# Two layers' block inversions, and some of layer 1's elementwise work, assigned to other engines

## The chip, the core and the metric

The kernel runs on one core of a Trainium2 chip. The metric is the device time of one execution in microseconds (us). The core has five engines that each run their own instructions in order and wait for one another by semaphores: TensorE (PE, with its weight loads shown as PEld), VectorE (DVE), ScalarE (ACT), GpSimd (POOL) and SyncE (SP, which here issues DMAs).

## The reference

The reference is one inference step of a two-layer hybrid decoder with a width of 1024. Layer 0 is a gated DeltaNet: an input projection, a short causal convolution on q, k and v, and a chunked delta rule in which every chunk solves a triangular system. Layer 1 is an RWKV-7 time mixing: five mixtures of a token with the one before it, projections r, k, v and z, a low-rank decay and rate, and a state update that the kernel also handles by chunks with triangular systems.

```
L = jnp.where(strict, jnp.einsum('nbhik,nbhjk->nbhij', kb, k) * decay, 0.0)
A = L + jnp.eye(chunk, dtype=L.dtype)
...
sol = lax.linalg.triangular_solve(A, rhs, left_side=True, lower=True, unit_diagonal=True)
...
xs = xn[None] + xx[None] * mu[:, None, None, :]
rkvz = jnp.einsum('sbtd,sde->sbte', xs[:4], w_rkvz)
...
kk = l2norm((k * k_k).reshape(B, T, H, N))
k = k * (1.0 + (a - 1.0) * k_a)
S = (S * d_t[:, :, None, :]
     + jnp.einsum('bhvk,bhk->bhv', S, -kk_t)[..., None] * b_t[:, :, None, :]
     + v_t[..., None] * k_t[:, :, None, :])
```

16 meta tokens, the prompt of 1024 tokens and 8 sample sequences of 8 tokens make 1104 columns, which the kernel handles in three segments of 384, 384 and 336.

## The kernel before, in words

**Products and splits.** A product in fp32 accuracy is three matmuls of halves: hi by x, lo by x, hi by x's lo. `split` (L135) makes the halves: ACT copies the hi half (L139), and POOL or DVE subtracts it from the value to get the lo half (L143). Weights come in as `wraw` (128 x 512 for half of a 128-column tile), and leave as `whi` and `wlo`.

**The inversions.** Each triangular system is handled as 32x32 blocks along the diagonal, which are inverted, and merged by PE. `inverse_steps` (L681) inverts up to 120 blocks at once, a block to a partition, in 31 steps. Step j makes a product `invtmp` of (31-j) x (j+1) elements to a partition (L689), and subtracts it from rows j+1 to 31 of `invT` (L691). Each of the 62 instructions needs the one before. `inverse_open` sets `invT` to the unit matrix (memsets L677 and L678 on POOL). Layer 0 has eight batches, one for each head pair, with 72 partitions; layer 1 has five, with 120 (the last 96): 13 x 31 = 403 steps.

**The order of layer 0.** The order of instructions on each engine is that in which the program emits them. Layer 0's work is emitted around one long stream of matmuls, the projections. After every six matmuls comes a gap, and a table (`Gaps`) tells which functions are called in it. Head pair j has 72 gaps from 24 + 72 j. In `prep_plan` (L731) the inversion's steps of pairs 1 to 6 are put one in 1.1 gaps, those of pairs 0 and 7 one in 0.8. Behind the last step, one gap apart, come four ACT copies of the inverse (L814), DMAs, and the merges of the system. Meanwhile `conv_plan` runs the convolution of the next tiles: a PE tile is copied to `raw` by ACT (L621), with the three columns before it copied by POOL (L620); ACT scales the first tap (`cvy`, L115), DVE adds the other three (L634), ACT takes a tanh, and DVE makes q, k or v (L641). The recurrence of the head pair before runs too: its `w` (ACT), `X` and `S` and `o` (DVE, L1038, L1071, L1092) lie between PE's `rA` products.

**The order of layer 1's projections.** `projections` (L2370) runs the r, v and z tiles, eight of each, as matmuls of 24 to a segment (`dense_tile`, L1436) with a gap after every 12, and a table `plan` of 180 gaps. `projection_weights` (L2334) gives `fetch` (the DMA) and `cast` (the split) of half a tile's weights; 48 halves are cast, three of them ahead of the first mixing. `mix_steps` (L2315) makes the token-shift mixture `mixs` (scaled on ACT, L2330 on DVE) and splits it, with the lo half alternately on POOL and DVE. `system_steps` (L1566) prepares one of 24 systems of a key head pair and segment; L1583, L1585 and L1592 on POOL are among its steps. Five systems make a batch, whose blocks are inverted by `system_inverse` (L1630), two steps to a gap over 16 gaps, and copied by ACT (L1638); 8 gaps later begin the merges. `late_weights` streams the z and output weights behind (`Stream`, split on POOL).

Of the kernel before, what the change touches and what calls it, by code (L numbers as in the profile page):

```python
# [88 lines left out]
class Builder:  # L89
# [496 lines left out]
    def conv_plan(self, ends, ft, dst, done=None):  # L586
# [75 lines left out]
        for s, e in enumerate(ends):  # L662
# [5 lines left out]
            if done is not None:  # L668
                L.put(e + 8, lambda s=s: done(s), 2.2)
        L.put(ends[2] + 3, ending, 2.5)  # L670
        L.put(ends[2] + 6, store, 3)
        return out
# [7 lines left out]

    def inverse_steps(self, A, nb, pool, T=None):  # L681

        nc = self.nc
        T = self.inverse_open(nb, pool) if T is None else T
        Tv = T.rearrange("p (i j) -> p i j", j=32)
        for j in range(31):
            n, m = 31 - j, j + 1
            tmp = self.t(pool, [128, 256], "invtmp", 1)[0:nb, 0:n * m].rearrange("p (n m) -> p n m", m=m)
            nc.vector.tensor_tensor(tmp, A[:, j, j + 1:32].unsqueeze(2).broadcast_to([nb, n, m]),  # L689
                                    Tv[:, j, 0:m].unsqueeze(1).broadcast_to([nb, n, m]), op=ALU.mult)  # L690
            nc.vector.tensor_tensor(Tv[:, j + 1:32, 0:m], Tv[:, j + 1:32, 0:m], tmp, op=ALU.subtract)  # L691
            yield Tv
# [38 lines left out]
    def prep_plan(self, j, B, G, o, pace):  # L731
# [67 lines left out]
        def invert():  # L799
# [5 lines left out]
            yield  # L805
            inv = self.inverse_steps(c.Av, 72, fp, T)
            for u in range(31):
# [758 lines left out]
    def system_steps(self, Q, B):  # L1566
# [15 lines left out]
        self.act(iD, cs, AF.Exp, scale=self.DEC)  # L1582
        nc.gpsimd.tensor_tensor(kk, kk, iD, op=ALU.mult)  # L1583
        yield
        nc.gpsimd.tensor_scalar(a, a, pc("rwkv_k_a"), self.omka[:, Q.p:Q.p + 1], op0=ALU.mult, op1=ALU.add)  # L1585
        yield
        ssp = self.ps("f", 2, "rss")
        for c in range(6):
            for h in (0, 1):
                b = slice(64 * h, 64 * h + 64)  # L1590
                self.mm(ssp[b, c:c + 1], sq[b, 64 * c:64 * c + 64], self.ones[b, 0:1])
        nc.gpsimd.tensor_tensor(a, a, k, op=ALU.mult)  # L1592
        nc.sync.dma_start(self.ald[Q.n], al)
# [36 lines left out]
    def system_inverse(self, B):  # L1630
# [3 lines left out]
        Av = B.A.rearrange("p (i s) -> p i s", s=32)  # L1634
        inv = self.inverse_steps(Av.rearrange("p i s -> p s i"), nb, pool)
        for Tv in inv:
# [697 lines left out]
    def projection_weights(self):  # L2334
# [11 lines left out]
        def cast(h):  # L2346
            whi[h], wlo[h] = (t(self.wp, [128, 4, 128], x, self.WB, F32R) for x in ("whi", "wlo"))
            self.split(raw.pop(h), whi[h], wlo[h])
        for h in (0, 1):
            fetch(h)  # L2350
        for h in (0, 1):
            cast(h)
            fetch(h + 2)
        cast(2)
        fetch(4)
        return tiles, whi, wlo, fetch, cast
# [13 lines left out]
    def projections(self, xa, xb, ip, opened, tiles, whi, wlo, fetch, cast):  # L2370
# [8 lines left out]
        def put(g, f, late=2):  # L2379
            plan[g].append((late, f))  # L2380
# [7 lines left out]
        def mixed(g, m, k, s, u):  # L2388
            c0, n = SEGS[s]
            if m == 3 and s == 2:  # L2390
                dst = [f[:, x, k, 0:n] for x in (0, 1)]
            else:
                dst = [x[k][:, c0:c0 + n] for x in xs[m]]
            g_ = self.mix_steps(m, k, SEGS[s], xb[k], dst, "pool" if u % 2 else "dve")
            steps(g, g_, 2)

        starts, g = [], 0
        for m, k in tiles:
            starts.append(g)
            g += 2 * count(m, k)  # L2400
        for h in range(3, 48):
            g = starts[h // 2]
# [3 lines left out]
            else:  # L2406
                put(max(0, g - 1) if h > 3 else 5, lambda h=h: cast(h), 0)
                put(g + 1 if h > 3 else 7, lambda h=h: h + 2 < 48 and fetch(h + 2), 0)

# [72 lines left out]

        for ti, (m, k) in enumerate(tiles):
            dst = {0: self.rd, 2: self.vd, 3: self.zd}[m]
            for s, (c0, n) in enumerate(SEGS[0:count(m, k)]):
                w = Halves(whi, 2 * ti), Halves(wlo, 2 * ti)
# [140 lines left out]
```

## Time and profile before

| | us |
|---|---|
| median of 3 runs | 2273.2 (2270.88 to 2274.19) |
| the profiled execution's own time | 2271.0 |
| its span | 2269.3 |
| PE busy | 2143.4 |
| DVE busy | 1584.5 |
| ACT busy | 1250.7 |
| POOL busy | 1004.0 |

The granted clock of PE is 0.98 on average. A page shows for every group of instructions the line, the engine, the operation, the tiles out<-in with their shapes, how many there are, busy time in us and the mean of one in ns, and behind a second bar the idle time of the engine just ahead of them with what ended it. A view of waits shows which engine, at which line, waited for which other: us in total, times, longest. A view of windows shows busy times in stretches of the span. A row of the timeline has the start, the length, the engine and the instruction, and in brackets the idle time before it.

### The profile page before, as it was taken

The numbers are of one execution on the slowest core, as the hardware profiler recorded it, in microseconds if no ns is written. First come the engines' busy times: TensorE is split into PE (matmuls) and PEld (weight loads), VectorE is DVE, ScalarE is ACT, GpSimd is POOL, SyncE is SP. The second block draws the span as 40 slices with busy tenths as digits, with TensorE's granted clock in tenths as the row PEclk, the third lists the DMA queues.
The fourth block names the chain that finished last, engine by engine and source line by source line (L and its number), as shares of the span: only waits on it lengthen the run. The fifth ranks groups of instructions, "written<-read, shape, count | busy, mean of one in ns | idle before, by whom it ended". The sixth has DMA issues, their size and how long they took to land.

```text
span 2269.3 us, 55274 instructions
## 1 busy us (share of the span) xinstructions
PE 2143.4 (94%) x20382; PEld 1966.5 (87%) x20382; DVE 1584.5 (70%) x4167; ACT 1250.7 (55%) x3631; POOL 1004.0 (44%) x1385
## 2 busy tenths in 40 slices
PE   7889999999999999989999999898999999999997
PEld 6788889889898989878999999798889977788886
DVE  6778788796969687885435762559887637667765
ACT  5536565556556565645433464644545456676763
POOL 4416262534335252614341442464543345566663
PEclk9999999999999999999999999999999999999997
DMA  3324242424333342436344234577786676655532
GB/s 113 79 67 127 65 124 67 110 80 109 85 105 99 81 122 71 114 78 184 95 143 106 70 103 169 167 237 196 206 247 155 157 186 155 173 162 158 168 118 91
DMA packets 495400, 291.61 MB, mean 129 GB/s; under 512 B 222345, under 2 KB 480506, under 8 KB 495130
## 3 DMA queue, kind: packets, MB, share of 16 engines
q1 hardware_dynamic: 495130, 288.08, 45.2%
q8 instruction: 161, 2.64, 0.5%
q14 instruction: 109, 0.89, 0.1%
HBM read 195.66 MB, written 92.30 MB: 127 GB/s over the span
## 4 chain that ended last, share of the span: by engine, by line
PE 46%; DVE 28%; issue 7%; ACT 6%; DMA 6%; POOL 3%; SPq 3%; DVEq 0%; POOLq 0%; ACTq 0%
PE d L129 10%; DVE invtmp L689 5%; PE rA L133 5%; DVE invT L691 5%; DVE cvy L634 4%; PE dz L129 4%; PE zo L129 3%; PE do L129 3%; PE rA L129 3%; PE dv L129 2%; PE fG L129 2%; PE dk L129 1%; DMA wraw<-in_gdn_w_out 1%; POOL wlo L143 1%; DVE E L765 1%
## 5 line engine op out<-in xcount | busy, mean ns | idle before, releaser
L143 POOL TENSOR_TENSOR wlo<-wraw,whi 128x512 fp32r<-128x512 f32 x238 | 321.1, 1350 | 490.1 <-ACT whi L139 391.5
L634 DVE SCALAR_TENSOR_TENSOR cvy<-raw,cw,cvy 128x408 f32<-128x408 f32 (+2 forms) x288 | 180.0, 625 | 35.8 <-ACT cvy L115 30.5
L689 DVE TENSOR_TENSOR invtmp<-invA,invT 72x31 f32<-72x31 f32 (+31 forms) x403 | 189.0, 469 | 15.6 <-POOL invT L678 10.1
L129 PE MATMUL d<-xc,whi 128*128 128x384 f32 (+1 forms) x640 | 181.4, 344 | 6.7 <-ACT xc L139 2.9
L691 DVE TENSOR_TENSOR invT<-invT,invtmp 72x31 f32<-72x31 f32 (+31 forms) x403 | 176.6, 438 | 14.1 <-DVE invtmp L689 0.2
L115 ACT ACTIVATE raw<-cvy 128x408 f32<-128x408 f32 (+2 forms) x96 | 49.8, 518 | 226.2 <-DVE cvy L634 178.0
L139 ACT CAST whi<-wraw 128x512 fp32r<-128x512 f32 x238 | 145.3, 612 | 26.0 <-DMA wraw<-in_rwkv_w_rkvz 12.5
L129 PE MATMUL dv<-xc,whi 128*128 128x384 f32 (+1 forms) x480 | 154.6, 343 | 0.0
L129 PE MATMUL dz<-xc,whi 128*128 128x384 f32 (+1 forms) x480 | 153.2, 342 | 0.0
L129 PEld LDWEIGHTS d<-xc,whi 128*128 128x128 f32 x640 | 118.0, 191 | 10.5 <-ACT xc L139 3.5
L129 PE MATMUL d<-xc,wlo 128*128 128x384 f32 (+1 forms) x320 | 105.4, 339 | 1.9 <-POOL wlo L143 1.8
L129 PE MATMUL d<-xa,whi 128*128 128x384 f32 (+1 forms) x336 | 101.2, 344 | 3.4 <-ACT whi L139 1.6
L129 PE MATMUL dz<-xa,whi 128*128 128x384 f32 (+1 forms) x288 | 102.3, 355 | 0.7 <-DVE zg L905 0.7
L129 PE MATMUL dv<-xa,whi 128*128 128x384 f32 (+1 forms) x288 | 100.9, 350 | 0.0
L1929 POOL TENSOR_SCALAR y<-y,mv,grs 128x64 f32<-128x64 f32 x132 | 81.1, 632 | 34.7 <-DVE grs L164 29.4
L129 PEld LDWEIGHTS dz<-xc,whi 128*128 128x128 f32 x480 | 90.4, 191 | 0.9
L129 PEld LDWEIGHTS dv<-xc,whi 128*128 128x128 f32 x480 | 89.0, 188 | 2.2 <-issue 1.6
L958 POOL TENSOR_SCALAR Sb<-Sb,eglb 128x128 f32<-128x128 f32 x128 | 90.4, 718 | 0.0
L160 POOL TENSOR_TENSOR ors<-ovar,cvals 128x6 f32<-128x6 f32 x24 | 35.8, 1492 | 118.9 <-DVE ovar L1121 118.6
L129 PE MATMUL d<-xl,whi 128*128 128x384 f32 (+1 forms) x256 | 82.8, 337 | 0.8 <-DVE xl L143 0.8
L129 PE MATMUL d<-xh,whi 128*128 128x384 f32 (+1 forms) x256 | 83.0, 336 | 0.1
L129 PE MATMUL d<-xh,wlo 128*128 128x384 f32 (+1 forms) x256 | 82.5, 336 | 0.0
(543 smaller groups left out, 7154.0 us busy)
## 6 DMA issues: line engine op xcount, KB each, us to landing
wraw<-in_gdn_w_in SPq DMA_DIRECT2D x96, 256.0 KB
wraw<-in_rwkv_w_rkvz SPq DMA_DIRECT2D x74, 256.0 KB
Sb<-in_state_gdn SPq DMA_DIRECT2D x64, 256.0 KB
wraw<-in_rwkv_w_o SPq DMA_DIRECT2D x48, 256.0 KB
E<-drow SPq DMA_DIRECT2D x24, 384.0 KB
attn<-drow SPq DMA_DIRECT2D x24, 384.0 KB
wraw<-in_gdn_w_out SPq DMA_DIRECT2D x36, 256.0 KB
out_s_gdn<-Sb SPq DMA_DIRECT2D x32, 256.0 KB
```

Of the source, the lines that this page charges most:

```text
L115: return self.nc.scalar.activation(out, in_, func, bias=bias, scale=scale, **kw)
L129: self.nc.tensor.matmul(out, lhsT, rhs, start=start, stop=stop)
L133: self.nc.tensor.matmul(out, lhsT, rhs, start=start, stop=True, skip_group_check=True)
L139: nc.scalar.copy(hi, x)
L143: e.tensor_tensor(lo, x, hi.bitcast(F32), op=ALU.subtract)
L160: self.nc.gpsimd.tensor_tensor(y, x, half.broadcast_to(sh), op=ALU.pow)
L634: nc.vector.scalar_tensor_tensor(ys[s][:, 0:wd(s)], raws[s][:, k:k + wd(s)], cw[k], ys[s][:, 0:wd(s)], op0=ALU.mult, op1=ALU.add)
L689: nc.vector.tensor_tensor(tmp, A[:, j, j + 1:32].unsqueeze(2).broadcast_to([nb, n, m]), Tv[:, j, 0:m].unsqueeze(1).broadcast_to([nb, n, m] ...
L691: nc.vector.tensor_tensor(Tv[:, j + 1:32, 0:m], Tv[:, j + 1:32, 0:m], tmp, op=ALU.subtract)
L765: nc.vector.scalar_tensor_tensor(E[:, tt, h], p_[s][:, 128 * tt:128 * tt + 128], c.bp[:, 3 * s + tt, h:h + 1], E[:, tt, h], op0=ALU.mult, ...
L958: nc.gpsimd.tensor_scalar(Sb[g][:, u], Sb[g][:, u], self.eglb[:, hv, 4 * g + u:4 * g + u + 1], None, op0=ALU.mult)
L1929: nc.gpsimd.tensor_scalar(y[:, q], y[:, q], mv[:, q, 0:1], P.rs[:, q:q + 1], op0=ALU.subtract, op1=ALU.mult)
```

## The change

The change has six parts.

1. The inversions of both layers run on GpSimd: 62 instructions of each of 13 batches leave DVE for POOL.
2. In `system_steps`, two products (L1583 and L1592) go from POOL to DVE, and the scaling of `a` (L1585) from POOL to ACT: 24 of each.
3. The lo halves of the r, v and z weights are made by DVE; four halves, and not three, are cast ahead of the first mixing, and two more at gaps 8 and 10.
4. The lo half of every mixture made in the gaps is made by DVE.
5. The first two r tiles run by segments: segment 0 of tile 0, segment 0 of tile 1, segment 1 of tile 0 and so on. All others run as before.
6. In the convolution, the transpose of the last three columns and its store come two gaps later.

```diff
@@ conv_plan
-        L.put(ends[2] + 3, ending, 2.5)
-        L.put(ends[2] + 6, store, 3)
+        L.put(ends[2] + 5, ending, 2.5)
+        L.put(ends[2] + 8, store, 3)
@@ inverse_steps
-    def inverse_steps(self, A, nb, pool, T=None):
+    def inverse_steps(self, A, nb, pool, T=None, eng=None):
+        v = eng or nc.vector
-            nc.vector.tensor_tensor(tmp, A[:, j, j + 1:32].unsqueeze(2).broadcast_to([nb, n, m]),
-                                    Tv[:, j, 0:m].unsqueeze(1).broadcast_to([nb, n, m]), op=ALU.mult)
-            nc.vector.tensor_tensor(Tv[:, j + 1:32, 0:m], Tv[:, j + 1:32, 0:m], tmp, op=ALU.subtract)
+            v.tensor_tensor(tmp, A[:, j, j + 1:32].unsqueeze(2).broadcast_to([nb, n, m]),
+                            Tv[:, j, 0:m].unsqueeze(1).broadcast_to([nb, n, m]), op=ALU.mult)
+            v.tensor_tensor(Tv[:, j + 1:32, 0:m], Tv[:, j + 1:32, 0:m], tmp, op=ALU.subtract)
@@ prep_plan, system_inverse
-            inv = self.inverse_steps(c.Av, 72, fp, T)
+            inv = self.inverse_steps(c.Av, 72, fp, T, nc.gpsimd)
-        inv = self.inverse_steps(Av.rearrange("p i s -> p s i"), nb, pool)
+        inv = self.inverse_steps(Av.rearrange("p i s -> p s i"), nb, pool, eng=nc.gpsimd)
@@ system_steps
-        nc.gpsimd.tensor_tensor(kk, kk, iD, op=ALU.mult)
+        nc.vector.tensor_tensor(kk, kk, iD, op=ALU.mult)
-        nc.gpsimd.tensor_scalar(a, a, pc("rwkv_k_a"), self.omka[:, Q.p:Q.p + 1], op0=ALU.mult, op1=ALU.add)
+        self.act(a, a, AF.Identity, scale=pc("rwkv_k_a"), bias=self.omka[:, Q.p:Q.p + 1])
-        nc.gpsimd.tensor_tensor(a, a, k, op=ALU.mult)
+        nc.vector.tensor_tensor(a, a, k, op=ALU.mult)
@@ projection_weights
-            self.split(raw.pop(h), whi[h], wlo[h])
+            self.split(raw.pop(h), whi[h], wlo[h], eng_lo='dve')
-        for h in (0, 1):
+        for h in range(4):
             cast(h)
             fetch(h + 2)
-        cast(2)
-        fetch(4)
@@ projections
-            g_ = self.mix_steps(m, k, SEGS[s], xb[k], dst, "pool" if u % 2 else "dve")
+            g_ = self.mix_steps(m, k, SEGS[s], xb[k], dst, "dve")
-        for h in range(3, 48):
+        for h, g in ((4, 8), (5, 10)):
+            put(g, lambda h=h: cast(h), 1)
+            put(g + 2, lambda h=h: fetch(h + 2), 0)
+        for h in range(6, 48):
-                put(max(0, g - 1) if h > 3 else 5, lambda h=h: cast(h), 0)
-                put(g + 1 if h > 3 else 7, lambda h=h: h + 2 < 48 and fetch(h + 2), 0)
+                put(g - 1, lambda h=h: cast(h), 0)
+                put(g + 1, lambda h=h: h + 2 < 48 and fetch(h + 2), 0)
-        for ti, (m, k) in enumerate(tiles):
+        order = [(ti, s) for s in range(3) for ti in (0, 1)]
+        order += [(ti, s) for ti in range(2, 24) for s in range(count(*tiles[ti]))]
+        for ti, s in order:
+            m, k = tiles[ti]
-            for s, (c0, n) in enumerate(SEGS[0:count(m, k)]):
+            for c0, n in SEGS[s:s + 1]:
```

How instructions stand on an engine now is shown at three places. A number behind a tile's name tells one tile from another, and the shape is that of the result; the lines behind L681 have one number more in the changed program.

The first place is POOL in layer 0, within the inversion of head pair 3. Before, with the copy L620 of the columns ahead of a segment and the split of a weight:

```order
L628 COPY last_4323<-raw_4254 128x24
L648 MEMSET Q_4327 128x48
L143 TENSOR_TENSOR wlo_4400<-wraw_4165,whi_4399 128x512
L620 COPY raw_4409<-raw_4254 128x3
L620 COPY raw_4489<-raw_4409 128x3
L630 COPY last_4323<-raw_4489 128x3
```

And now:

```order
L692 TENSOR_TENSOR invT_4234<-invT_4234,invtmp_4377 72x28x4
L143 TENSOR_TENSOR wlo_4398<-wraw_4165,whi_4397 128x512
L620 COPY raw_4407<-raw_4254 128x3
L690 TENSOR_TENSOR invtmp_4414<-invA_4232,invT_4234 72x135
L692 TENSOR_TENSOR invT_4234<-invT_4234,invtmp_4414 72x27x5
L690 TENSOR_TENSOR invtmp_4445<-invA_4232,invT_4234 72x156
L692 TENSOR_TENSOR invT_4234<-invT_4234,invtmp_4445 72x26x6
L690 TENSOR_TENSOR invtmp_4463<-invA_4232,invT_4234 72x175
L692 TENSOR_TENSOR invT_4234<-invT_4234,invtmp_4463 72x25x7
L690 TENSOR_TENSOR invtmp_4476<-invA_4232,invT_4234 72x192
L692 TENSOR_TENSOR invT_4234<-invT_4234,invtmp_4476 72x24x8
L620 COPY raw_4489<-raw_4407 128x3
```

Between the two L620 copies, which stood one behind the other, there are now four steps of the inversion.

The second place is POOL in layer 1's projections, from the third batch's opening memset on. Before, with the steps of `system_steps`, a mixture's split and the weights' splits:

```order
L678 MEMSET invT_21038 120x32
L1592 TENSOR_TENSOR slda_20855<-slda_20855,sldk_20857 128x384
L1576 MEMSET sal_21125 128x6
L1583 TENSOR_TENSOR skk_21124<-skk_21124,sldcs_20965 128x384
L143 TENSOR_TENSOR xc_104<-mixs_21104,xc_104 128x384
L1585 TENSOR_SCALAR slda_20967<-slda_20967,pcol_331,omka_83 128x384
L143 TENSOR_TENSOR wlo_21184<-wraw_21023,whi_21183 128x512
L1592 TENSOR_TENSOR slda_20967<-slda_20967,sldk_20969 128x384
L1576 MEMSET sal_21272 128x6
```

And now, the batch's fourth step and those behind it:

```order
L690 TENSOR_TENSOR invtmp_21081<-invA_20891,invT_21038 120x112
L692 TENSOR_TENSOR invT_21038<-invT_21038,invtmp_21081 120x28x4
L1577 MEMSET sal_21125 128x6
L690 TENSOR_TENSOR invtmp_21138<-invA_20891,invT_21038 120x135
L692 TENSOR_TENSOR invT_21038<-invT_21038,invtmp_21138 120x27x5
L690 TENSOR_TENSOR invtmp_21141<-invA_20891,invT_21038 120x156
L692 TENSOR_TENSOR invT_21038<-invT_21038,invtmp_21141 120x26x6
```

Only the memset of `sal` still lies among the inversion's steps; the other work has left POOL.

The third place is PE at the start of layer 1's projections, at the end of the second run of 24 matmuls. Before, with the output tile `d`, the activations' halves and the weights' halves:

```order
L129 MATMUL d_3246_18475<-xa_7_100,wlo_3209_18282 128x384
L129 MATMUL d_3246_18475<-xa_7_100,whi_3208_18281 128x384
L129 MATMUL d_3248_18502<-xa_7_100,whi_3205_18275 128x336
L129 MATMUL d_3248_18502<-xa_7_100,wlo_3206_18276 128x336
L129 MATMUL d_3248_18502<-xa_7_100,whi_3205_18275 128x336 x2
```

And now:

```order
L129 MATMUL d_3249_18481<-xa_7_100,wlo_3215_18294 128x384
L129 MATMUL d_3249_18481<-xa_7_100,whi_3214_18293 128x384
L129 MATMUL d_3251_18508<-xa_7_100,whi_3205_18275 128x384
L129 MATMUL d_3251_18508<-xa_7_100,wlo_3206_18276 128x384
L129 MATMUL d_3251_18508<-xa_7_100,whi_3205_18275 128x384 x2
```

The third run was tile 0's last segment (336 columns) and is now tile 0's second segment (384 columns), since tile 1's first segment has come between.

## The prediction, made before the changed kernel had run

> **What bounds the kernel now.** I read the page's busy times first, then the windows in which an inversion runs, then what TensorE (PE) waits for in each. On the page:
>
> ```profile
> PE 2143.4 (94%) x20382; PEld 1966.5 (87%) x20382; DVE 1584.5 (70%) x4167; ACT 1250.7 (55%) x3631; POOL 1004.0 (44%) x1385
> L143 POOL TENSOR_TENSOR wlo<-wraw,whi 128x512 fp32r<-128x512 f32 x238 | 321.1, 1350 | 490.1 <-ACT whi L139 391.5 <-DVE bv L883 34.6 <-DVE E L765 18.9
> L689 DVE TENSOR_TENSOR invtmp<-invA,invT 72x31 f32<-72x31 f32 (+31 forms) x403 | 189.0, 469 | 15.6 <-POOL invT L678 10.1
> L691 DVE TENSOR_TENSOR invT<-invT,invtmp 72x31 f32<-72x31 f32 (+31 forms) x403 | 176.6, 438 | 14.1 <-DVE invtmp L689 0.2
> ```
>
> PE is busy 94% of the span, so all its idle time is 2269.3 - 2143.4 = 126 us; what edits to other engines can gain is in that, and where matmuls follow one another more slowly than elsewhere. The inversions cost VectorE (DVE) 189.0 + 176.6 = 365.6 us; GpSimd (POOL) is the emptiest engine. But an average says nothing of the stages. The windows view with each engine's busy time, in which the columns are the window, its length, then PE, PEld, DVE, ACT and POOL: the inversions of head pairs 0, 3 and 7 in layer 0, then the third and the fifth of layer 1:
>
> ```profile
> 108.00:146.00 38.00, 30.97 (x224) 28.04 (x224) 36.12 (x89) 9.92 (x23) 9.48 (x20) 0.96 0.25 67
> 334.00:390.00 56.00, 53.61 (x405) 50.43 (x404) 51.38 (x136) 30.90 (x103) 15.73 (x25) 1.00 0.23 69
> 954.00:1004.00 50.00, 43.91 (x335) 39.86 (x334) 46.05 (x119) 25.47 (x83) 12.79 (x20) 1.00 0.21 61
> 1646.00:1696.00 50.00, 47.05 (x636) 42.48 (x634) 46.48 (x92) 22.18 (x53) 25.11 (x28) 0.97 0.85 233
> 1761.00:1797.00 36.00, 36.00 (x411) 33.13 (x410) 33.85 (x75) 16.03 (x42) 13.68 (x22) 1.00 0.53 151
> ```
>
> The same view of the inversion's instructions alone, head pair 3, DVE's busy time:
>
> ```profile
> 334.00:390.00 56.00, 25.27 (x62) 1.00 0.23 69
> ```
>
> DVE is over 90% busy in every one of these windows, half of it by the inversion, but PE still runs at 53.6 of 56 us for head pair 3. What PE waits for there (us in total, times, longest):
>
> ```profile
> PE rA L129 <- ACT w L115: 1.4, 2, 1.0
> PE rA L129 <- DVE o L1092: 1.0, 2, 0.7
> ```
>
> Only 2.4 us in a window of head pairs 1 to 6 are there to be had. Pair 0 (first fence, us 105 to 147) and pair 7 (second, 953 to 1005) have more:
>
> ```profile
> PE f L126 <- DVE vt L641: 5.6, 3, 3.2
> PE f L126 <- DVE raw L608: 1.1, 1, 1.1
> ```
>
> ```profile
> PE rA L129 <- DVE X L1038: 2.4, 2, 1.2
> PE rA L129 <- ACT w L115: 2.2, 1, 2.2
> PE rA L129 <- DVE o L1092: 1.2, 1, 1.2
> ```
>
> That is 6.7 and 5.8 us.
>
> **What one inversion costs on POOL.** A batch is 31 products and 31 subtractions. A step's tile has (31-j)(j+1) elements to a partition, 5456 over the 31 steps. No row shows these on POOL, so I fit a line through POOL's own two-input rows, the split above (512 elements, 1350 ns) and the mask product, and take the product, both of whose operands are broadcast, from the row of such a product:
>
> ```profile
> L1607 POOL TENSOR_TENSOR sqs<-sqs,m_strs 128x64 f32<-128x64 f32 x8 | 3.1, 391 | 6.2 <-DVE sqs L1605 6.2
> L1981 POOL TENSOR_TENSOR ue<-UV,bmask 128x512 f32<-128x512 f32 x8 | 8.4, 1045 | 1.2 <-PE drsw L129 1.2
> ```
>
> (1350 - 391) / 448 = 2.14 ns an element and 254 ns a start; for the product (1045 - 254) / 512 = 1.545. Subtractions: 31 x 0.254 + 5456 x 0.00214 = 7.9 + 11.7 = 19.6 us. Products: 7.9 + 8.4 = 16.3. Every instruction now waits for the one before it on its own engine. Two dependent POOL instructions in the timeline show what that costs:
>
> ```profile
> 330.53 0.95 POOL L677 MEMSET invT<- 72x1024 f32 x1
> 331.54 0.15 POOL L678 MEMSET invT<- 72x32 f32 x1
> ```
>
> The second starts 0.06 us after the first ends; 62 x 0.06 = 3.7 us. In all 39.6 us a batch, 1.28 us a step, against 25.3 on DVE. Bounds: 32 us if products and subtractions both go at 1.545 ns and the wait is nothing, 50 if they go at the split's 2.14 and the operands' strides add a quarter. I take 39.6, since each term has its own nearest row.
>
> The Trainium skill ("GPSIMD Engine Reference", section 3.1) speaks against this move: it measures a two-input elementwise operation on GpSimd at 1.96 times VectorE's time, and names VectorE for such work. By that rule the batch would take an estimated 25.3 x 1.96 = 49.6 us, near my upper bound, and the sum for pairs 1 to 6 would fall to the slower rival; no run here has shown it yet.
>
> **Layer 0.** Pairs 1 to 6: POOL has 15.7 us of other work in the window, so 39.6 + 15.7 = 55.3 of 56 us: it just fits, with nothing left over. DVE falls to 51.4 - 25.3 = 26.1. So the waits on DVE go and those on ACT (whose w waits for DVE) mostly too: at best -2.4. POOL also holds the copies L620 and weight splits L143, which now queue behind one or two inversion steps of 1.3 us; ScalarE (ACT), in order, stands at the first tap's scaling until L620 is done, and its `w` is queued behind that. I give 1 us of it back: -1.5 a pair, -9 for six. Bounds: -15 (all waits gone), +24 (the rival, +4 each).
>
> Pair 0: 39.6 + 9.5 = 49.1 us in a window of 38, 11 late. The 6.7 us of waits on DVE go, and the system's copies and merges, which PE needs for pair 0's first segment, come 11 us later: 11 - 7 = +4. Bounds -7 (lateness hidden) and +12. Pair 7: 39.6 + 12.8 = 52.4 in 50, 2.4 late, and of 5.8 us of waits I count 3.4 as gone: -1. Bounds -5.8 and +6. Moving the closing transpose of the convolution two gaps back costs nothing: its result goes only to an output, and PE has other matmuls at both places.
>
> **Layer 1's start.** The r tiles begin while xc and xl of the last segment are still being made. PE's timeline:
>
> ```profile
> 1451.34 0.42 PE L129 MATMUL d<-xc,whi 128*128 128x336 f32 x1 [2.62 <-ACT xc L139]
> ...
> 1456.87 0.93 PE L129 MATMUL d<-xc,whi 128*128 128x336 f32 x2 [2.83 <-POOL xc L143]
> ...
> 1458.15 0.48 PE L129 MATMUL d<-xh,whi 128*128 128x336 f32 x1
> 1458.43 0.48 PE L129 MATMUL d<-xh,wlo 128*128 128x336 f32 x1
> ...
> 1462.63 0.34 PE L129 MATMUL d<-xa,wlo 128*128 128x384 f32 x1
> 1462.80 0.34 PE L129 MATMUL d<-xa,whi 128*128 128x384 f32 x1
> ```
>
> 5.5 us of idle time, and behind it matmuls that start every 0.28 us instead of 0.17 for a larger tile, until about 1461. So segment 2 of the first tile, 24 matmuls of 336 columns, runs from 1451.34 - 2.62 = 1448.7 to about 1461.3, 12.6 us; at the later rate it would be 24 x 0.17 x 336/384 = 3.6 us. Some 9 us are lost. With segments 0 and 1 of tile 1 put ahead of it, segment 2 comes 2 x 24 x 0.17 = 8 us later, and its splits have that time. DVE also makes xa, xc and xl at 0.57 us where POOL takes over 1 (the row for DVE is below). I count -8; bounds -10 and 0 (the weights' halves for tiles 1 and 2 are then late, since four are cast at once at the start).
>
> **The rest of layer 1.** POOL's work in the third batch's window, by kind:
>
> ```profile
> L143 POOL TENSOR_TENSOR wlo<-wraw,whi 128x512 fp32r<-128x512 f32 x5 | 6.8, 1369 | 2.1 <-ACT whi L139 2.1
> L1592 POOL TENSOR_TENSOR slda<-slda,sldk 128x384 f32<-128x384 f32 x6 | 6.4, 1071 | 0.2
> L1583 POOL TENSOR_TENSOR skk<-skk,sldcs 128x384 f32<-128x384 f32 x5 | 6.2, 1233 | 15.4 <-ACT sldcs L115 7.7 <-issue 4.8 <-ACT sTT L115 2.9
> L1585 POOL TENSOR_SCALAR slda<-slda,pcol,omka 128x384 f32<-128x384 f32 x5 | 4.2, 833 | 0.0
> L143 POOL TENSOR_TENSOR xc<-mixs,xc 128x384 fp32r<-128x384 f32 x2 | 2.2, 1112 | 0.1
> L1576 POOL MEMSET sal<- 128x6 f32 x5 | 0.5, 109 | 7.2 <-ACT sal L115 7.2
> ```
>
> All but the last of these leave POOL, so 39.6 + 0.5 = 40 of 50 us there. What is moved costs, on DVE and ACT:
>
> ```profile
> L143 DVE TENSOR_TENSOR xl<-mixs,xh 128x384 fp32r<-128x384 f32 x11 | 6.3, 573 | 0.0
> L115 ACT ACTIVATE mixs<-xb,omu 128x384 f32<-128x384 f32 x15 | 9.1, 613 | 2.9 <-DVE xl L143 1.1 <-POOL xc L143 0.9 <-DVE xa L143 0.5
> ```
>
> DVE loses 365.6 - 8 x 25.3 = 163 us and takes 48 weight splits (at most 0.573 x 512/384 = 0.76 us each, 36.7), 21 mixing splits and 48 products (69 x 0.573 = 39.5): 76 us, 87 less. ACT takes 24 x 0.613 = 14.7 us at 22 of 50 us busy; it hides there. PE's waits from 1500 to 1800 that this can reach:
>
> ```profile
> PE fL L129 <- DVE sqs L1605: 2.8, 3, 2.1
> PE d L129 <- POOL wlo L143: 2.7, 5, 0.9
> ```
>
> Against them stand new waits: DVE's L1584, in order, waits for ACT's exponential, with weight splits queued behind it; the memset `sal` stands behind up to two steps on POOL (2.6 us), and DVE's next line waits for it; and in the fifth window 40 us of inversion have 36. So 5.5 us to be had and some 4 late at the end: -2, bounds -12 and +15.
>
> **Sum.** -9 + 4 - 1 - 8 - 2 = -16 us. The profiled execution took 2271.0 us (span 2269.3), 2.2 below the median of the three runs, so 2255 for such a run and 2273.2 - 16 = 2257 us for the median. With half of each term's doubt this case runs from 2240 to 2268.
>
> **The rivals.**
> *Everything is gained*: all the waits that the terms name go, and nothing is late: -15 - 7 - 6 - 10 - 7 = -45, 2228 us. For it: DVE has 30 us to spare in each window. Against it: POOL has none.
> *No change*: layer 0 nets nothing (pairs 1 to 6 keep their waits, now on POOL; pair 0 costs 8), and layer 1's start gives the 8: 2273 us.
> *Part*: the start's 8 us, but 2 of it lost again where DMA is 85% busy in the third window: -6, 2267.
> *Slower: POOL and DVE shut each other out.* The timeline has it:
>
> ```profile
> 240.72 0.41 DVE L689 TENSOR_TENSOR invtmp<-invA,invT 72x256 f32<-72x256 f32 x1
> 240.79 1.47 POOL L143 TENSOR_TENSOR wlo<-wraw,whi 128x512 fp32r<-128x512 f32 x1 [5.51 <-ACT whi L139]
> 241.17 1.37 DVE L691 TENSOR_TENSOR invT<-invT,invtmp 72x256 f32<-72x256 f32 x1
> ```
>
> Beside POOL's split DVE's subtraction took 1.37 us where the product of the same size took 0.41: it ended when the split did. POOL busy all through would hold up DVE's two-input work of the window (some 28 instructions, 15 us), and be held up by it. Then POOL needs 55 + 8 to 15 us for 56, weight splits and L620 copies come late, and PE waits: 4 us for each of six pairs, 10 for pair 0, 5 for pair 7, less the start's 8: +31, 2304 us. It decides once a step of the inversion takes over about 1.45 us on average, (56 - 15.7) / 31 = 1.30 and 5 us of slack before the first merge; I have 1.28. Against it: most of POOL's rows already hold such overlaps, since DVE is busy beside them. The Trainium skill ("GPSIMD Engine Reference", section 1) says the same of the cause: GpSimd shares its SBUF interfaces with VectorE and contends with instructions of two SBUF inputs. The trace agrees, by the 1.37 us.
>
> **How the numbers follow.** A measurement of this kernel can tell about 0.2%, 4.5 us, from no change. Forecast 0.47, everything gained 0.12, part 0.05: faster 0.64. No change 0.11. The slower rival 0.25. The range reaches from 2236 (half of the best case left out) to 2292 (of the slower rival, whose price may be anywhere from +6 to +57, some 0.14 left out). The likeliest sign's own range is 2228 to 2267.
>
> **What would show it.** Right: an inversion's window on POOL holds 62 instructions in 37 to 43 us; DVE near 26 us in the window of pair 3; PE's waits on `o` and `w` under 1 us there; no idle time over 1 us near 1451 and 1457; pair 0's window longer by some 11 us. Wrong: steps over 1.45 us, waits of PE on `wlo` L143 or of ACT on `raw` L620 in each of layer 0's windows, a DVE that is as busy as before with longer instructions, or idle time at layer 1's start that only comes later.

## The result and the profile after

The changed kernel took 2263.9 us in the median of 9 runs (2254.5 to 2269.1), the kernel before 2272.5 (2268.6 to 2274.3) beside it: a ratio of 0.9954, interval 0.9938 to 0.9970. It is faster by 8.6 us in the medians, some 10 by the ratio; 16 were forecast, with 2257 us and a range of 2236 to 2292. That range is 56 us wide and holds "no change" too. The profiled execution took 2265.0 us, 6.0 less than that of before. The page of the changed kernel, in whose lines L690 and L692 are the product and the subtraction of the inversion:

```profile
span 2263.3 us, 55248 instructions
...
PE 2152.0 (95%) x20382; PEld 1980.7 (88%) x20382; DVE 1379.1 (61%) x3478; ACT 1266.0 (56%) x3655; POOL 1315.5 (58%) x2050
...
L692 POOL TENSOR_TENSOR invT<-invT,invtmp 72x31 f32<-72x31 f32 (+31 forms) x403 | 255.1, 633 | 31.6
L634 DVE SCALAR_TENSOR_TENSOR cvy<-raw,cw,cvy 128x408 f32<-128x408 f32 (+2 forms) x288 | 203.2, 706 | 73.0 <-ACT cvy L115 67.4
L690 POOL TENSOR_TENSOR invtmp<-invA,invT 72x31 f32<-72x31 f32 (+31 forms) x403 | 231.0, 573 | 24.8 <-DMA invA<-ltd 1.5
```

The work went where the change says: DVE 1584.5 to 1379.1 us, POOL 1004.0 to 1315.5. PE is busy 9 us longer with the same 20382 matmuls, and that is the first sign that something happened to its clock.

A total can't show where a change of 6 us comes from, so I compared when the same matmul starts in both timelines, at marks between the stages:

| mark | before | after | difference |
|---|---|---|---|
| pair 0, a v tile | 102.7 | 100.7 | -2.0 |
| behind pair 0's merges, a k tile | 173.0 | 189.7 | +16.7 |
| behind pair 6's merges, a k tile | 906.9 | 914.0 | +7.1 |
| behind pair 7's merges, output tile | 1049.6 | 1062.2 | +12.6 |
| ahead of layer 1's projections | 1437.3 | 1449.6 | +12.3 |
| after the first two r tiles | 1463.7 | 1462.2 | -1.4 |
| a little later | 1512.1 | 1514.3 | +2.2 |
| fourth batch of layer 1 | 1713.1 | 1708.4 | -4.7 |
| near the end | 2202.3 | 2195.9 | -6.3 |

So the six pairs in the middle gained 9.6 us (9 forecast). Pair 0 lost 18.7 from the first mark to the second, where 4 were forecast. Pair 7 lost 5.5, where 1 was to be gained. Layer 1's start gained 13.7, of which 3.7 were lost again (8 forecast), and the rest of layer 1 and what follows gained 8.5 (2 forecast). The marks come from one profiled execution of each kernel.

Pair 3's inversion on POOL, in the windows view with all engines and then with its own instructions:

```profile
352.00:405.00 53.00, 51.87 (x397) 48.98 (x396) 35.23 (x72) 28.67 (x94) 46.80 (x82) 1.00 0.21 63
```

```profile
352.00:405.00 53.00, 36.20 (x62) 1.00 0.21 63
```

62 instructions take 36.2 us, 1.17 us a step; the sum had 35.9 and 3.7 of waits. Idle time ahead of the two lines above is 31.6 + 24.8 us for 806 instructions, 0.07 us each where I had 0.06. The price was right. DVE fell less than I expected: to 35 us and not to 26. The window holds 72 of its own instructions, where before it had 74 in the 26 us beside the inversion, so it is the instructions that grew: L634 took 625 ns on average over the whole kernel and now takes 706. PE's waits there, by the view of waits:

```profile
PE rA L129 <- DVE o L1093: 0.5, 1, 0.5
PE rA L129 <- ACT w L115: 0.5, 1, 0.5
```

That is 1.0 us in place of 2.4. Now pair 0. PE's waits between 60 and 215 us:

```profile
PE f L126 <- POOL vt L648: 5.2, 2, 3.3
PE flast L126 <- POOL last L630: 3.9, 1, 3.9
...
PE uY L129 <- DMA T1n<-g_t: 2.0, 2, 1.5
```

A memset of 48 zero columns and a copy of three, each about half a microsecond of work or less, stand behind inversion steps in POOL's queue, and PE waits 9.1 us for them. That replaces the 6.7 us of waits on DVE. Between the first two marks PE is idle for 12.4 us where it was idle for 7.4, so waits make 5.0 of the 18.7 us. The rest is elsewhere: no wait is listed between 160 and 190, but the windows show the clock (the third column from the end), for the changed kernel and then for the kernel before:

```profile
130.00:140.00 10.00, 4.97 (x21) 4.71 (x21) 4.41 (x7) 3.38 (x8) 9.29 (x14) 0.83 0.00 0
140.00:150.00 10.00, 8.36 (x42) 8.36 (x43) 1.52 (x3) 0.45 (x1) 8.90 (x19) 0.83 0.33 93
150.00:160.00 10.00, 8.04 (x68) 7.42 (x67) 2.23 (x4) 5.93 (x14) 5.36 (x12) 1.00 0.40 86
160.00:170.00 10.00, 9.90 (x145) 8.80 (x145) 2.45 (x6) 2.39 (x7) 0.00 (x0) 0.51 0.49 116
170.00:180.00 10.00, 10.00 (x96) 8.40 (x95) 2.13 (x5) 1.57 (x4) 0.00 (x0) 0.50 0.01 2
180.00:190.00 10.00, 10.00 (x54) 9.03 (x53) 2.75 (x8) 2.58 (x7) 3.46 (x7) 0.63 0.12 30
```

```profile
150.00:160.00 10.00, 10.00 (x180) 8.93 (x180) 4.67 (x10) 4.24 (x12) 2.62 (x3) 1.00 0.49 95
160.00:170.00 10.00, 10.00 (x145) 8.66 (x144) 4.01 (x11) 2.44 (x6) 0.00 (x0) 1.00 0.25 72
170.00:180.00 10.00, 10.00 (x65) 9.63 (x64) 5.10 (x13) 5.79 (x19) 7.65 (x13) 1.00 0.44 120
```

From 160 to 187 us the array ran at half its clock while pair 0's merges went through it: 4.9 + 5.0 + 3.7 = 13.6 us lost. In the kernel before the same merges ran at 1.00. Pair 7 shows it in little, after and then before:

```profile
1000.00:1020.00 20.00, 17.62 (x95) 17.25 (x96) 10.24 (x24) 10.77 (x32) 12.69 (x24) 0.83 0.22 61
1020.00:1040.00 20.00, 16.25 (x222) 14.08 (x222) 8.06 (x20) 8.10 (x23) 4.53 (x7) 0.85 0.55 138
1040.00:1060.00 20.00, 19.50 (x184) 18.05 (x185) 9.44 (x26) 10.44 (x35) 6.19 (x13) 0.90 0.44 127
```

```profile
1000.00:1020.00 20.00, 18.06 (x180) 16.41 (x180) 10.97 (x31) 10.65 (x31) 3.73 (x4) 0.91 0.51 118
1020.00:1040.00 20.00, 18.58 (x246) 16.73 (x244) 9.35 (x23) 11.22 (x33) 5.75 (x16) 1.00 0.47 134
```

3.4 + 3.0 + 2.0 = 8.4 us of clock lost, against 1.8 in the two windows of before.

### The profile page after: what moved, and what is told of

It reads as the page before. It is cut to its first block, busy times and chain, and to the rows that moved or that the text cites. A ratio compares the mean times of both kernels' runs of the same rounds, so it can differ in the third digit from the quotient of the medians.

```text
span 2263.3 us, 55248 instructions
## 1 busy us (share of the span) xinstructions
PE 2152.0 (95%) x20382; PEld 1980.7 (88%) x20382; DVE 1379.1 (61%) x3478; ACT 1266.0 (56%) x3655; POOL 1315.5 (58%) x2050
## 4 chain that ended last, share of the span: by engine, by line
PE 47%; POOL 20%; DVE 11%; ACT 7%; DMA 6%; issue 5%; SPq 2%; POOLq 0%; DVEq 0%; ACTq 0%
PE d L129 13%; POOL invT L692 7%; POOL invtmp L690 6%; PE rA L133 5%; PE dz L129 4%; PE zo L129 3%; PE do L129 3%; POOL wlo L143 3%; DVE cvy L634 2%; PE rA L129 2%; PE dk L129 2%; PE fG L129 2%; DMA wraw<-in_gdn_w_out 1%; POOL ors L160 1%; DVE E L766 1%
## 5 line engine op out<-in xcount | busy, mean ns | idle before, releaser
L143 POOL TENSOR_TENSOR wlo<-wraw,whi 128x512 fp32r<-128x512 f32 x190 | 247.6, 1304 | 253.0 <-ACT whi L139 216.0
L692 POOL TENSOR_TENSOR invT<-invT,invtmp 72x31 f32<-72x31 f32 (+31 forms) x403 | 255.1, 633 | 31.6
L634 DVE SCALAR_TENSOR_TENSOR cvy<-raw,cw,cvy 128x408 f32<-128x408 f32 (+2 forms) x288 | 203.2, 706 | 73.0 <-ACT cvy L115 67.4
L690 POOL TENSOR_TENSOR invtmp<-invA,invT 72x31 f32<-72x31 f32 (+31 forms) x403 | 231.0, 573 | 24.8 <-DMA invA<-ltd 1.5
L115 ACT ACTIVATE raw<-cvy 128x408 f32<-128x408 f32 (+2 forms) x96 | 49.6, 517 | 188.6 <-DVE cvy L634 125.1
```

What stands on the lines that cost most here:

```text
L115: return self.nc.scalar.activation(out, in_, func, bias=bias, scale=scale, **kw)
L143: e.tensor_tensor(lo, x, hi.bitcast(F32), op=ALU.subtract)
L634: nc.vector.scalar_tensor_tensor(ys[s][:, 0:wd(s)], raws[s][:, k:k + wd(s)], cw[k], ys[s][:, 0:wd(s)], op0=ALU.mult, op1=ALU.add)
L690: v.tensor_tensor(tmp, A[:, j, j + 1:32].unsqueeze(2).broadcast_to([nb, n, m]), Tv[:, j, 0:m].unsqueeze(1).broadcast_to([nb, n, m]), op=AL ...
L692: v.tensor_tensor(Tv[:, j + 1:32, 0:m], Tv[:, j + 1:32, 0:m], tmp, op=ALU.subtract)
```

## The experiments

Each kernel ran in 4 to 12 executions beside the kernel before on the same chip. The kernel before itself took 2267.5 to 2274.9 us (medians) in these three sets of runs, so kernels are compared by their ratio to it. Each has one profile, of one execution.

**1. Pair 0 back on VectorE.** In `prep_plan`:

```diff
-            inv = self.inverse_steps(c.Av, 72, fp, T, nc.gpsimd)
+            inv = self.inverse_steps(c.Av, 72, fp, T, nc.gpsimd if j else nc.vector)
```

> Only head pair 0's inversion goes back to VectorE; all else as changed. Theory A (pair 0 costs the gain): in the changed kernel's profile PE falls 16.7 us behind the kernel before between 128 and 190 us, 9 us of it new waits on POOL's small jobs queued behind the inversion (memset vt L648, copy last L630), 13.7 us a stretch of 27.3 us at half granted clock that follows; both go: 2263.9 - 16 = 2248 us (2243 to 2253), no half-clock stretch over 7 us between 120 and 190. Theory B (the half-clock stretch has nothing to do with pair 0, it comes from the z tiles and merges whatever runs the inversion): the stretch stays, 2255 to 2262.

Measured: 2249.6 us, ratio 0.9890 (0.9874 to 0.9907), against 0.9954 for the whole change: 14.6 us less. Two of its windows:

```profile
160.00:170.00 10.00, 10.00 (x143) 8.66 (x142) 4.01 (x11) 2.59 (x7) 0.00 (x0) 1.00 0.22 67
170.00:180.00 10.00, 10.00 (x66) 9.63 (x66) 5.10 (x13) 5.80 (x18) 7.80 (x14) 1.00 0.45 120
```

The clock is 1.00. Theory A held: pair 0's inversion on GpSimd cost more than the whole change gained.

**2. Pairs 0 and 7 back on VectorE.** As above with `nc.gpsimd if 0 < j < 7 else nc.vector`.

> Head pairs 0 and 7 on VectorE again, the six between and layer 1 on GpSimd. Theory A: as with pair 0 alone, and between 955 and 1045 us the 5.7 us that the changed kernel loses (half clock for 17.1 us there, against 3.4 before: 6.8 us) come back too: 2248 - 6 = 2242 us (2237 to 2248). Theory B: pair 7's loss is the end of layer 0, where z tiles run out and the clock falls anyway: no change against pair 0 alone.

Measured: 2243.9 us, 0.9863 (0.9846 to 0.9880), 6.1 us less than with pair 0 alone by the ratios. As forecast by A. The two intervals overlap, but both kernels ran in the same set of runs, and all four executions of this one (at most 2245.6) are below all five of the other (at least 2247.7).

**3. Small jobs to VectorE, inversions as changed.** Five lines of `conv_plan`, as

```diff
-                nc.gpsimd.tensor_copy(x[:, 0:3], prev(s - 1))
+                nc.vector.tensor_copy(x[:, 0:3], prev(s - 1))
...
-                    nc.gpsimd.memset(d[:, n:384], 0.0)
+                    nc.vector.memset(d[:, n:384], 0.0)
```

> All inversions stay on GpSimd; the convolution's small jobs go from GpSimd to VectorE: the copies of 3 columns L620, of last L628 and L630, the memsets L609 and L648. Theory A1 (pair 0's loss comes from small jobs queued behind inversion steps): PE's waits on POOL vt and POOL last (9.1 us from 60 to 215, 2.4 from 950 to 1050) go and the half-clock stretch with them; ACT's wait for raw L620 goes in pairs 1 to 6 as well: 2264 - 18 = 2246 us (2238 to 2254). Theory A2 (the inversion of pair 0 is itself late, 45 us in place of 38, and PE idles for its merges): the stretch stays, 2256 to 2264.

Measured: 2266.5 us, 0.9962 (0.9943 to 0.9982): no better than the change. Theory A1 fell. PE's waits from 60 to 215 us in this kernel:

```profile
PE dz L129 <- POOL wlo L143: 5.1, 1, 5.1
PE uY L129 <- DMA T1n<-g_t: 3.1, 2, 2.8
```

The small jobs no longer hold PE up, and the next thing in POOL's queue, a weight split, does; the merges' data come late as before. The half clock stays too, by the windows:

```profile
160.00:170.00 10.00, 9.84 (x143) 8.54 (x142) 2.74 (x7) 1.91 (x6) 0.00 (x0) 0.53 0.48 119
170.00:180.00 10.00, 10.00 (x102) 8.83 (x99) 2.13 (x5) 2.06 (x5) 0.00 (x0) 0.50 0.01 2
```

So it is theory A2: the inversion itself is late.

**4. Filler matmuls ahead of pair 0's merges.** Behind the merges' plan:

```diff
+        if j == 0:
+            for u in range(7, 12):
+                L.put(i0 + u, lambda: self.busy("f", 2, 10), 0.9)
```

> As changed, with fifty matmuls more whose result nobody reads, ten in each of five gaps from just ahead of pair 0's first merge; 6 us of work at full clock. Theory G (the half-clock stretch is kept up because the merges' small matmuls don't count as enough work, after idle time has let the clock fall): the stretch of 27.3 us goes or is under 11 us, 2264 - 13.7 + 6 = 2256 us (2251 to 2261). Theory H (the clock follows something else, as time since the start): the stretch stays and the filler costs 6 to 12 us: 2270 to 2276.

Measured: 2259.6 us, 0.9948 (0.9929 to 0.9968). The windows of its profile:

```profile
150.00:160.00 10.00, 10.00 (x74) 10.00 (x73) 1.51 (x2) 6.05 (x14) 5.44 (x12) 1.00 0.40 87
160.00:170.00 10.00, 10.00 (x191) 9.47 (x190) 2.62 (x7) 0.64 (x2) 0.00 (x0) 1.00 0.34 75
170.00:180.00 10.00, 10.00 (x150) 9.18 (x141) 2.00 (x6) 3.33 (x9) 0.00 (x0) 1.00 0.16 44
```

The inversion is as late as in the changed kernel, and the clock stays at 1.00: theory G's forecast held for the clock, and H fell. The time hardly followed, 1.4 us by the ratios, inside both intervals, since the filler is itself work in PE's path, and twice as much as I had counted. In the profile the fifty calls are a hundred matmuls of 12 us:

```profile
L129 PE MATMUL fbusy<-ident 128*128 128x128 f32 x100 | 12.0, 275 | 0.0
```

Twelve us of filler for 13.6 of clock leave next to nothing, as measured. So clock and lateness are two things. But the filler does two things at once: PE's idle time at the first merges is gone (10.00 of 10 us busy from 150 to 160, against 8.04), and large matmuls stand among the small ones. Which of the two kept the clock up, this run can't tell. Small merges alone do not bring it down: in the kernel before they ran at 1.00 without a filler.

The Trainium skill ("TensorE: Matmul & The Clock Gate", Part 1) tells of a gate that halves the clock after an idle window of some 3.4 us and frees it after one busy window. The halving agrees (0.50). That one busy window frees it agrees twice in the changed kernel's profile: the 0.83 of the windows from 130 to 150 us are two stretches of 0.17 x 10 / 0.5 = 3.4 us at half clock, behind PE's waits of 3.9 and 3.3 us, and no merge runs in them. It does not agree for the third stretch: PE was 99 to 100% busy from 160 to 180 us at 0.51 and 0.50, and the idle time ahead of it was only 1.5 and 0.4 us. By number, most of what ran there were the merges' matmuls of 32x32 and 64x64; by time, over half were the projections' large ones. Whether the small ones are what kept the gate down was not tried by itself.

**5. All of layer 0 on VectorE.** `inverse_steps(c.Av, 72, fp, T)` for every pair.

> All eight inversions of layer 0 on VectorE again; layer 1 and the convolution's two gaps as changed. Theory I (the 1.6 us that each of pairs 1 to 6 gains in the profiles come from the inversion on GpSimd): against pairs 0 and 7 alone on VectorE (2243.9 us) 6 x 1.6 = 9.7 us are lost: 2253.6 us (2250 to 2257). Theory E (they come from the transpose that was put two gaps later, which no longer stands in PE's way): 2244 us.

Measured: 2251.9 us, 0.9914 (0.9889 to 0.9939), 11.6 us more than with pairs 1 to 6 on GpSimd. Theory I held by the time, but not in full: by the start of the same matmuls this kernel still gains 3.1 us on the kernel before over the five pair lengths from 250.5 to 870.6 us, 0.6 us a pair, with every inversion on VectorE. Run 8 follows that up.

**6. The r tiles one after the other.** `order = [(ti, s) for ti in range(24) for s in range(count(*tiles[ti]))]`.

> The first two r tiles run one after the other again; casts, splits and inversions as changed. Theory R (the order by segments made the gain at layer 1's start, 13.7 us between 1437 and 1462 in the profiles, of which 3.7 are lost again by 1512): 2264 + 10 = 2274 us (2268 to 2278), idle time of PE over 2 us near the tile's third segment. Theory S (the faster splits on VectorE and the fourth half cast ahead made it): 2264 +- 3.

Measured: 2274.1 us, 0.9993 (0.9978 to 1.0007), 8.9 us more than the change. Theory R held. PE's waits from 1437 to 1490 us, first in the changed kernel, then in this one:

```profile
PE flora L129 <- ACT ev L115: 1.6, 3, 0.7
PE d L129 <- POOL xa L143: 0.8, 1, 0.8
```

```profile
PE d L129 <- ACT xc L139: 3.1, 2, 2.6
PE flora L129 <- ACT ev L115: 1.1, 3, 0.7
PE d L129 <- POOL xa L143: 0.9, 1, 0.9
```

With the plain order the wait for ACT's xc is back, while the 2.8 us for xc's lo half are not. POOL still makes that half in this kernel and in the changed one, since the mixtures of the start are not among those that moved. But before, the half stood on POOL behind L1583, a weight's split and L1585; these have left POOL, which now waits for ACT's xc instead.

**7. Layer 1's inversions.** Three kernels from that of run 2. In the first the five inversions of layer 1 go back to VectorE, with all else that moved left where it is:

```diff
-        inv = self.inverse_steps(Av.rearrange("p i s -> p s i"), nb, pool, eng=nc.gpsimd)
+        inv = self.inverse_steps(Av.rearrange("p i s -> p s i"), nb, pool)
```

> From the kernel with pairs 0 and 7 on VectorE: layer 1's five inversions go back to VectorE too, the moved splits and products stay there. Theory D (GpSimd's inversions make room on VectorE for the splits): VectorE then has 46.5 us and some 11 of moved work for 50 us in a window: 2243.9 + 10 to 25 = 2254 to 2269. Theory N (layer 1 gains by its start alone, the place of its inversions does not matter): 2244 +- 3.

Measured: 2236.2 us, 0.9837 (0.9814 to 0.9860), 5.9 us less than with them on GpSimd. Both theories fell. The two intervals overlap, so by these times alone the gain is not clear. But the kernel of run 5 (0.9914) and the third one below (0.9856) differ by the same edit, and their intervals do not overlap: the inversions are better on VectorE, full as it is. In the profiles the kernel with them on VectorE gains 7 us on the other between the marks at 1512 and 2202 us, in both comparisons. Little of that is idle time of PE: from 1512 to 1713 this kernel takes 189.3 us, 4.5 of them idle, and that of run 2 takes 196.6, 5.8 idle; most of the rest is the granted clock, 0.99 against 0.96. The windows of its first two batches, VectorE's inversion alone:

```profile
1505.00:1549.00 44.00, 21.17 (x62) 0.00 (x0) 1.00 0.82 236
1561.00:1603.00 42.00, 21.17 (x62) 0.00 (x0) 1.00 0.78 231
```

21.2 us a batch, where the kernel before needed 28 to 36 for the same instructions, as in its third and fifth batch:

```profile
1646.00:1696.00 50.00, 36.03 (x62) 0.97 0.85 233
1761.00:1797.00 36.00, 27.83 (x62) 1.00 0.53 151
```

What differs beside them is POOL, which is now all but idle (0.9 and 0.4 us busy in the two windows). In the second kernel the lo halves and the three steps go back to POOL, beside the inversions:

> From the kernel with pairs 0 and 7 on VectorE: the lo halves of weights and of every second mixture, and the three steps of system_steps, go back to GpSimd, where layer 1's inversions stay. Theory Q (GpSimd can hold either but not both): 40 + 25 us of work for windows of 50, weight halves late at each batch: 2243.9 + 20 to 60 = 2264 to 2304, with PE waiting for POOL wlo L143. Theory F (the other work fits between the batches): 2244 to 2249.

Measured: 2297.3 us, 1.0114 (1.0093 to 1.0134), Theory Q. PE's waits from 1440 to 1850 us are led by

```profile
PE d L129 <- POOL wlo L143: 38.3, 12, 8.9
```

POOL can hold the inversions or the splits. For the third kernel, I took out part 1 altogether:

> The change without its first part: all thirteen inversions on VectorE, the other five parts as changed. Theory P (the other parts make the whole gain, and the inversions on GpSimd cost pairs 0 and 7 and layer 1): layer 0 on VectorE stood at 0.9914 of the kernel before, layer 1's inversions back on VectorE took 0.0026 more off: 0.9888, or some 2246 us beside 2271 (2240 to 2251), 18 less than the whole change. Theory V (VectorE, which then has the inversions and the moved work, is full): 2258 to 2275.

Measured: 2235.8 us, 0.9856 (0.9833 to 0.9879). It is theory P, and more than it said: without the part that gives the change its name, the change is 1.4% faster than before and not 0.5%. Against the kernel with pairs 1 to 6 on GpSimd (0.9837) the intervals overlap; whether those six are worth their place is not settled by the times. In the profiles they are worth some 5.5 us (run 8 has the windows).

**8. What else moved.** From the kernel with 0.9837, the three steps of `system_steps` back on POOL and ACT's scaling with them:

> From the kernel with pairs 1 to 6 alone on GpSimd (2236 us beside 2271): the three steps of system_steps go back to GpSimd. Theory C (GpSimd's two-input instructions lengthen VectorE's inversion, which took 28 to 36 us a batch in the kernel before and 21.2 with GpSimd idle): batches of 24 to 29 us on VectorE, 2238 to 2244. Theory L (VectorE is relieved of 27 us and ACT of 15, which is worth as much): 2232 to 2236.

Measured: 2239.8 us, 0.9874 (0.9854 to 0.9894). The inversion's windows for the first two batches:

```profile
1501.00:1549.00 48.00, 30.60 (x62) 0.00 (x0) 0.96 0.69 205
1561.00:1607.00 46.00, 28.54 (x62) 0.00 (x0) 0.96 0.71 214
```

Then, instead, the lo halves of the weights and of every second mixture back on POOL:

> From the same kernel: the lo halves of the r, v and z weights and of every second mixture go back to GpSimd, the fourth half cast ahead and the order by segments stay. Theory C: batches of 24 to 31 us on VectorE, and at layer 1's start PE waits for GpSimd's splits again: 2241 to 2250. Theory L: VectorE is relieved of 49 us: 2231 to 2236.

Measured: 2242.0 us, 0.9884 (0.9866 to 0.9902), and the inversion's windows:

```profile
1503.00:1550.00 47.00, 25.98 (x62) 0.00 (x0) 1.00 0.77 227
1564.00:1610.00 46.00, 26.25 (x62) 0.00 (x0) 0.89 0.71 210
```

21.2 us with POOL idle; 28.5 to 30.6 with the three steps on POOL beside it, 26 with the splits. The kernel with the three steps shows it within itself: beside its last two batches POOL has 0.2 us of work and none, and they took 21.2 and 20.9. Theory C held in the traces both times. By the time, the kernel with the splits on POOL is clear of 0.9837 and that with the three steps is not quite. Last, the two gaps in the convolution:

```diff
-        L.put(ends[2] + 5, ending, 2.5)
-        L.put(ends[2] + 8, store, 3)
+        L.put(ends[2] + 3, ending, 2.5)
+        L.put(ends[2] + 6, store, 3)
```

> From the same kernel: the transpose of the last three columns and its store at their old places, two gaps earlier. Theory T (with all of layer 0 on VectorE PE still gained 0.6 us a pair on the kernel before: the transpose stood in PE's way): 8 x 0.6 = 5 us more, 2239 to 2243. Theory Z (its place costs nothing, as predicted): 2235 to 2238.

Measured: 2241.6 us, 0.9882 (0.9862 to 0.9901), 10 us more by the ratios, and the intervals just miss each other. By the start of the same matmuls, pairs 1 to 6 gain 1.6 us each with the later transpose and 0.25 without it. PE's waits in pair 3's window (336 to 389 us):

```profile
PE flast L126 <- POOL last L630: 2.1, 1, 2.1
PE rA L129 <- DVE o L1093: 0.5, 1, 0.5
```

The transpose at its old place waits 2.1 us for a copy of three columns, L630, which is queued behind inversion steps. Theory T held, with a larger size and for another reason than 0.6 us: with the inversion on GpSimd the two gaps are what makes the move pay. One window over pairs 1 to 6, between the same two matmuls, shows it for four kernels: the kernel before; this one (inversions on GpSimd, transpose at its old place); run 7's third one (inversions on VectorE, transpose later); and the one with both moved:

```profile
173.00:906.90 733.90, 710.64 (x6058) 657.45 (x6056) 587.11 (x1664) 426.58 (x1383) 311.05 (x487) 1.00 0.36 96
172.90:905.00 732.10, 708.84 (x6057) 658.96 (x6055) 495.24 (x1292) 426.67 (x1383) 511.51 (x859) 1.00 0.36 96
175.20:905.50 730.30, 710.21 (x6057) 658.07 (x6055) 584.90 (x1664) 426.52 (x1383) 310.20 (x487) 1.00 0.36 97
173.90:898.70 724.80, 709.51 (x6057) 657.93 (x6055) 493.77 (x1292) 427.08 (x1383) 513.39 (x859) 1.00 0.36 97
```

PE is idle for 23.3, 23.3, 20.1 and 15.3 us. The inversions on GpSimd alone take nothing off, the later transpose alone 3.2 us, and both together 8.0. These windows hold 7.3 of the 10 us; where the other 3 lie is not shown.

## Why the prediction was right, and where it was not

The sign and the range held, and the size just within a factor of two (8.6 us of 16). Term by term, the sum came near by luck as much as by reasoning:

- **The price on POOL** was 39.6 us a batch, 35.9 of it busy; measured 36.2 in layer 0 and 37 to 41 in layer 1, with waits of 0.07 us. In layer 0 a line through two rows of the same engine was good to 1%; in layer 1 the batch was up to 15% dearer. The Trainium skill's ratio ("GPSIMD Engine Reference", section 3.1) gave 49.6 us, and layer 0's trace does not agree: 36.2 / 25.3 = 1.43. In layer 1 it comes nearer: 37 to 41 us on POOL against 21.2 on VectorE beside an idle POOL is 1.75 to 1.95.
- **Pairs 1 to 6**, -9: measured -9.6. In pair 3 the waits fell about as said, from 2.4 to 1.0 us. But "moving the closing transpose two gaps back costs nothing" missed the point of that edit: it is right that it costs nothing, yet with it undone 1.4 of the 1.6 us a pair are gone (run 8). I asked what it costs to move it, and not what would wait on POOL if it stayed.
- **Pair 0**, +4: measured +18.7, the term that failed. The lateness was sized as 11 us less the 7 of waits that go. The window grew by 7 us, from 38 to 45, and the first merge started 4 us later; but the waits on DVE were replaced by waits on POOL. PE's idle time rose by 5.0 us, so that the +4 looks right there by luck, as both its halves were off. The step that failed is what the sum left out: 13.6 us came from the clock, a column that I had quoted for every window (1.00, 0.96) and not put into any term. Runs 1 and 4 show both halves of it.
- **Pair 7**, -1: measured +5.5, of which 6.6 are clock (8.4 less 1.8).
- **Layer 1's start**, -8: measured -13.7 at 1463.7 us and -10 by 1512; run 6 gives 8.9 for the order by segments. That DVE makes the last segment's lo halves at 0.57 us was wrong for the start: POOL still makes every second one there.
- **The rest**, -2: measured -8.5 with what follows, 6.9 of it by 1713 us. Of the two waits that were to be had, the 2.8 us for `sqs` went, and the 2.7 us for `wlo` came back as 2.7 us on DVE; waits that I had not counted, for `whi`, `xa`, `xl` and `invtmp`, fell by 4.3 us, one for a DMA (`sTT`) rose by 3.0, and PE's idle time from 1512 to 1713 us fell by 4.8. DVE took up some 90 us of moved work where I had 76: a weight's lo half took 850 ns, and I had put it at 760 at most. What the sum missed is what POOL's work costs DVE. I quoted the row in which one subtraction took 1.37 us beside a split, and used it for a rival alone, and "half of it by the inversion" passed over the third batch of layer 1, where the inversion had 36.0 of DVE's 46.5 us. The same row says what taking work off POOL is worth: VectorE's inversion goes from 28 to 36 us to 21.2 (run 7), which the changed kernel, with its inversions on POOL, can't use. Putting the inversions there costs it some 7 us in layer 1 by the traces. In the groups of instructions of the kernel of run 2, in its second batch (1554 to 1608 us, inversions on GpSimd), VectorE's splits and `sal`, and then the splits in the second batch of the kernel with layer 1's inversions on VectorE:

```profile
L143 DVE TENSOR_TENSOR wlo<-wraw,whi 128x512 fp32r<-128x512 f32 x6 | 5.3, 890 | 0.7 <-ACT whi L139 0.7
...
L1582 DVE SCALAR_TENSOR_TENSOR sal<-sldk,pcol,sal 128x384 f32<-128x384 f32 x5 | 4.5, 893 | 13.0 <-POOL sal L1577 13.0
```

```profile
L143 DVE TENSOR_TENSOR wlo<-wraw,whi 128x512 fp32r<-128x512 f32 x5 | 3.4, 684 | 0.0
```

A split takes 890 ns in place of 684, and VectorE waits 13.0 us in that window for the memset of `sal`, one of the new waits that I had named (2.6 us each).
- **The slower rival** did not decide: a step took 1.17 us of POOL, below its 1.45. Its mechanism is there: L634 took 706 ns for 625, and a batch on POOL took 37 to 41 us in layer 1 beside DVE's moved work and 33 to 36 where that work was on POOL itself (run 7's second kernel). Its price was not.

Two misses of opposite sign, pair 0 and 7 (+21 more than forecast) and layer 1 (-9), made a median that looks closer than the terms were.

## What to carry to other kernels

Moving work to the emptiest engine is judged by the fullest window and by what is queued behind it there, not by its average: here a copy of three columns behind inversion steps was worth more than the step that it waited for. Where two engines slow each other, work taken off the one may pay on the other, and the move in the opposite direction is worth a run: the part that the change was named for could be left out, and the rest was three times as good. And PE's idle time is not its only price: here 2 us of it at the start of pair 0's merges were followed by 13.6 us lost to the clock.

## What the hardware showed that was not expected

The half clock outlasted the idle time ahead of it by far: two waits of 1.5 and 0.4 us at pair 0's first merges, then 27 us at 0.50 with PE 99 to 100% busy, and none of it when a hundred filler matmuls were put among them. In the same profile, the longer waits of 3.9 and 3.3 us were each followed by 3.4 us at half clock and no more. The times of the changed kernel go with its mean clock, from 2254.5 us at 0.978 to 2269.1 at 0.968 over nine runs; whether it is this stretch that differs among them is not shown, since one was profiled. With pairs 0 and 7 on VectorE four runs lay between 2242.7 and 2245.6.

GpSimd's two-input instructions stretched the same 62 VectorE instructions from 21.2 us to 26 and 31, by which of GpSimd's work stood beside them; with GpSimd idle the two windows quoted gave 21.17 us both.
